# GpSimd's arithmetic moved to VectorE in a two-layer diffusion backbone, with five first feature chunks on TensorE

## The chip, the cores and the metric

The kernel runs on one core of a Trainium2 chip. The metric is the device time of one execution in microseconds; less is better. Engines are named as in the profile: PE is TensorE's matmuls and PEld its weight loads, DVE is VectorE, ACT is ScalarE, POOL is GpSimd, SP is the queue that issues most of the loads. L529 means line 529 of the kernel before.

## The reference, cut to what matters

Two layers over 640 tokens of 1024 features: 128 context tokens (modulated by one condition) and 512 latent tokens (modulated by another). A layer is a feed-forward sublayer, a mixer of four branches with attention, and a second feed-forward sublayer. Each sublayer is wrapped in two norms:

```
def pre(x_, s):
    return rmsnorm(x_, g_pre[l, s]) * (1 + mods[:, 3*s + 1]) + mods[:, 3*s]
f = swiglu(pre(x, 0), w_ffn_gu[l, 0], w_ffn_dn[l, 0])          # (silu(g) * u) @ w_dn
x = x + 0.5 * mods[:, 2] * rmsnorm(f, g_post[l, 0])
m = token_mix(pre(x, 1), ...)   # pooling, spatial gating, latent attention, short conv,
x = x + mods[:, 5] * rmsnorm(m, g_post[l, 1])   # merged by sigmoid gates, one output projection
mods = silu(cond) @ w_mod + b_mod               # nine sections of 1024 per layer
```

## The kernel before, in words

Features lie on partitions, in 8 chunks of 128 (`KC`), and tokens along the free dimension (640, in two halves of 320, `HW`). Every float32 operand is split in a high part (a ScalarE cast) and a low part (a VectorE subtraction, `split`, L242 and L243), and each product is made of three matmuls. Weights come by SP's queue one unit ahead, are split when a task begins (`run`, `advance`), and then the task's function issues its matmuls. All engines work in the order in which the program issues.

**Start** (`start`, L1432 on). The squares of x are summed, and the first two modulation sections are worked out chunk by chunk. Chunks in `BY_PE` use 16 small matmuls each on TensorE (`mod_pe`); the others use dot products along the free dimension (`mod_ve`): three on VectorE (L1496) and one as a GpSimd product (L1502) that ScalarE sums up. `hi` makes the high part of the modulated input (GpSimd product with the norm's factor at L1521, two ScalarE passes, a cast), `lo` the low part (L1528). A `hook` issues these steps between the matmuls of the first three weight units (`first`), so that chunk k is made while chunk k-1 is multiplied.

**Boundaries** (`boundary`, `chain`). Between two sublayers the tokens go half by half. While TensorE runs the tail of one sublayer for the second half, the generator `chain` of the first half is stepped by hand-written counts (`STEPS`): it normalises the branch output f, adds it to x (L450), sums the squares of the new x (L425), and makes the high and low part of the next input (L488 to L509). The second half's chain runs under the next sublayer's head. In `chain`, `scaled` (L414) is a GpSimd product with the norm's factor; a chunk that is `solo` or `alone` has a VectorE form without it. `evac_branch` sums the squares of f (GpSimd, L529), deferred to the next task by `later`. There are five boundaries and a last chain that has a `post` and no `pre`.

**Feed-forward** sublayers make whole-chunk sums of the two input parts for a seven-product scheme (`sums`, L637 on GpSimd). **The mixer** has, in its front, the kv and query norms (`norms`), the rotary key (`rope`), the pooling windows (`windows`, `pooling`), and the short convolution; then 16 attention steps between which gates and branches are filled in, whose outputs are merged by additions (L1127 and L1131 on GpSimd).

GpSimd's queue also issues the transfers of the intermediate results to and from memory.

Of the kernel before, what the change touches and what calls it, by code (L numbers as in the profile page):

```python
# [9 lines left out]
F32 = mybir.dt.float32  # L10
# [18 lines left out]
BY_PE = (0, 2, 4)  # L29
# [51 lines left out]
class Kernel:  # L81
# [319 lines left out]
    def chain(self, hf, ahead, kind, post=None, pre=None, out=None):  # L401
# [15 lines left out]

        accs = (acc,) if ahead else (self.ssq[:, s], acc)
        n = len(accs)

        def square(c, q):
            a = accs[c % n]
            nc.scalar.activation(a if c < n else q, self.x[:, c, s], AF.Square)
            if c >= n:
                (nc.vector if ahead or c % 2 else nc.gpsimd).tensor_add(a, a, q)  # L425

        if post is not None:
# [5 lines left out]
            solo = lambda c: pre is None and not ahead and c in (0, 3)  # L433
# [35 lines left out]

        alone = lambda c: c % 2 == 1  # L470
# [45 lines left out]
    def evac_branch(self, ps, c, hf):  # L516
# [6 lines left out]
        def squares():  # L523
            if c == 0:
                nc.scalar.activation(ssq[:, s], f[:, c, s], AF.Square)
            else:
                q = self.t3()
                nc.scalar.activation(q, f[:, c, s], AF.Square)
                nc.gpsimd.tensor_add(ssq[:, s], ssq[:, s], q)  # L529
# [61 lines left out]
    def ffn(self, l, st, mod_todo, first=False):  # L591
# [35 lines left out]
        def sums():  # L627
# [6 lines left out]
            for k in range(KC // 2):  # L634
                a1, a2, s31, s24 = (self.t6() for _ in range(4))
                for d, c in ((a1, k), (a2, KC // 2 + k)):
                    nc.gpsimd.tensor_add(d, f(self.h[0][:, c, :]), f(self.h[1][:, c, :]))  # L637
# [212 lines left out]
    def mixer(self, l):  # L850
# [36 lines left out]
        def raw_out(name, o, ps, hf):  # L887
# [4 lines left out]
            if sq is not None:  # L892
                d = Z[:, Z_SQ + sq + s.start:Z_SQ + sq + s.stop]
                if name == "cq1":
                    q = self.t3()
                    act.activation(q, ps[:, hf, :HW], AF.Square)
                    pool.tensor_add(d, d, q)
# [49 lines left out]
        def norms():  # L947
# [13 lines left out]
            rope(kr, Z[:, Z_KR:Z_KR + T], segs, pool)  # L961
# [26 lines left out]
        def windows(cc):  # L988
# [3 lines left out]
            pool.tensor_add(s1[:, 1:PADW], x[:, 0:PADW - 1], x[:, 1:PADW])  # L992
            if cc == 0:
                pool.tensor_add(s2[64:128, 2:PADW - 1], s1[64:128, 1:PADW - 2], s1[64:128, 3:PADW])
            else:
                pool.tensor_add(s2[:, 2:PADW - 1], s1[:, 1:PADW - 2], s1[:, 3:PADW])
                pool.tensor_add(s1[:, 4:PADW - 3], s2[:, 2:PADW - 5], s2[:, 6:PADW - 1])
                pool.tensor_add(s2[64:128, 8:PADW - 7], s1[64:128, 4:PADW - 11], s1[64:128, 12:PADW - 3])
            lo, hi = PO, PADW - PO
            pool.tensor_mul(ic[0:64, lo:hi], s1[0:64, lo:hi], ic[0:64, lo:hi])  # L1000
            pool.tensor_mul(ic[64:128, lo:hi], s2[64:128, lo:hi], ic[64:128, lo:hi])

        def pooling(cc):
# [3 lines left out]
            for o, b, n in ((PO, 0, TP), (SO, TP, TS)):  # L1007
                pool.tensor_sub(t[:, b:b + n], ic[:, o:o + n], x[:, o:o + n])
# [62 lines left out]
        def att_begin():  # L1071
# [16 lines left out]
            for b in range(2):  # L1088
                kh, kl = M["kt"][b]
                act.copy(kh[64:96, :], kr[64:96, :])  # L1090
                (dve, pool)[b].tensor_sub(kl[64:96, :], kr[64:96, :], kh[64:96, :].bitcast(F32))
# [18 lines left out]
        def branch(c, i):  # L1110

            def fn(*ws):
# [12 lines left out]
                elif i == 3:  # L1125
                    mg = M["mg"]
                    pool.tensor_add(mg, M["mt"], t)  # L1127
                    pool.dma_start(self.d_acc[c], mg)
                elif i == 1:
                    mg = M["mg"] = M["acc"].pop(c)  # L1130
                    pool.tensor_add(mg, mg, t)  # L1131
# [293 lines left out]
    def build(self):  # L1425
# [6 lines left out]
        def start():  # L1432
# [67 lines left out]
            def mod_ve(c):  # L1500
                t = sp.tile([P, D], F32, tag="pr", name=self.nm("t"), bufs=2)
                nc.gpsimd.tensor_mul(t, loads[0, c], sc[:, 0, :])  # L1502
                dot(1, c, 0)
                dot(1, c, 1)
# [212 lines left out]
```

## Time and profile before

| | |
|---|---|
| median of 3 runs | 3194.71 us (3193.94 to 3196.09) |
| the profiled execution's own time | 3198.12 us |
| its span (first to last instruction) | 3196.3 us |
| mean granted TensorE clock | 0.98 |

The profiled execution is one run more; its span leaves out 1.8 us around the first and the last instruction.

### The profile page before, as it was taken

To read this page: it belongs to the slowest core of one execution; us is meant where nothing else is said; L and a number is where in the kernel's file an instruction comes from. 1 tells how busy PE (TensorE), PEld (TensorE's weight loads), DVE (VectorE), ACT (ScalarE), POOL (GpSimd) and SP (SyncE) were. 2 spreads that over 40 slices of the span, in tenths; PEclk is the share of its full clock that TensorE was granted. 3 is DMA by queue.
4 is the path that set the end of the run, shared out by engine and by line. 5 is a ranking of instruction groups with operands and counts; after the bars stand their busy time and mean duration, and the time that the engine had idled before them with its cause. 6 is when DMAs were issued, how large, how long until landed. Compare 5 with 4: busy or idle time off the path is not lost. (4 is left out here: it accounts for less than half of the span.)

```text
span 3196.3 us, 51354 instructions
## 1 busy us (share of the span) xinstructions
PE 3036.4 (95%) x20278; PEld 2985.0 (93%) x20278; DVE 2353.4 (74%) x3522; ACT 1432.2 (45%) x2535; POOL 653.7 (20%) x601
## 2 busy tenths in 40 slices
PE   7899998999999979999989999989999999899997
PEld 6899997899999979999979999989999998899997
DVE  8978768876656598888688888678666666876665
ACT  4244356454432454443554443563444324544444
POOL 4200025500011242000441000444000113310014
PEclk9999999999999999999999999999999999999999
DMA  4436553311234445446545536542212444445344
GB/s 180 169 120 185 160 170 125 130 59 57 69 107 150 157 152 185 128 136 173 186 151 180 151 114 170 192 160 74 67 49 67 151 139 158 140 141 137 97 141 149
DMA packets 140213, 433.45 MB, mean 136 GB/s; under 512 B 16834, under 2 KB 34050, under 8 KB 139076
## 3 DMA queue, kind: packets, MB, share of 16 engines
q1 hardware_dynamic: 119380, 351.34, 32.8%
q0 software_dynamic: 20304, 78.66, 9.1%
q8 instruction: 159, 2.61, 0.3%
q14 instruction: 82, 0.67, 0.1%
q10 hardware_dynamic: 288, 0.17, 0.0%
HBM read 377.51 MB, written 52.59 MB: 135 GB/s over the span
## 5 line engine op out<-in xcount | busy, mean ns | idle before, releaser
L243 DVE TENSOR_TENSOR wl<-raw,wh 128x1024 fp32r<-128x1024 f32 (+3 forms) x525 | 601.8, 1148 | 380.2 <-ACT wh L242 371.9
L311 PE MATMUL ps<-act,wh 128*128 128x320 f32 x2816 | 567.6, 312 | 33.2 <-ACT act L242 15.4
L242 ACT CAST wh<-raw 128x1024 fp32r<-128x1024 f32 (+3 forms) x525 | 481.1, 919 | 72.6 <-PE ps L311 32.9
L311 PEld LDWEIGHTS ps<-act,wh 128*128 128x128 f32 x2816 | 455.8, 190 | 41.8 <-ACT act L242 18.2
L665 PE MATMUL ps<-s,wh 128*128 128x320 f32 x1920 | 442.9, 310 | 0.5 <-DVE t L689 0.4
L311 PE MATMUL ps<-slotA,wh 128*128 128x320 f32 x1312 | 368.3, 318 | 16.9 <-ACT wh L242 14.0
L311 PE MATMUL ps<-slotD,wh 128*128 128x320 f32 x1312 | 352.5, 316 | 19.5 <-DVE slotD L1528 15.3
L311 PE MATMUL ps<-slotA,wl 128*128 128x320 f32 x1312 | 365.2, 316 | 5.1 <-DVE wl L243 4.8
L311 PE MATMUL ps<-slotB,wh 128*128 128x320 f32 x1312 | 363.5, 315 | 3.0 <-DVE slotB L509 1.6
L311 PE MATMUL ps<-slotC,wh 128*128 128x320 f32 x1312 | 352.0, 316 | 7.4 <-ACT wh L242 3.2
L311 PE MATMUL ps<-act,wl 128*128 128x320 f32 x1408 | 353.7, 311 | 0.0
L375 DVE CUSTOM_DVE_ANT_0 t<-wm,sc,par 128x1024 bf16<-128x1024 f32 x256 | 330.2, 1327 | 12.9 <-DMA wm<-in_w_mod 12.5
L665 PEld LDWEIGHTS ps<-s,wh 128*128 128x128 f32 x1920 | 325.9, 188 | 3.0 <-issue 2.6
L665 PE MATMUL ps<-s,wl 128*128 128x320 f32 x960 | 296.6, 309 | 0.0
L311 PEld LDWEIGHTS ps<-slotA,wh 128*128 128x128 f32 x1312 | 240.5, 193 | 19.9 <-ACT wh L242 15.1
L311 PEld LDWEIGHTS ps<-slotD,wh 128*128 128x128 f32 x1312 | 236.4, 193 | 22.8 <-DVE slotD L1528 16.5
L311 PEld LDWEIGHTS ps<-slotA,wl 128*128 128x128 f32 x1312 | 240.8, 193 | 9.6 <-DVE wl L243 8.4
L311 PEld LDWEIGHTS ps<-act,wl 128*128 128x128 f32 x1408 | 246.3, 190 | 0.2
L311 PEld LDWEIGHTS ps<-slotC,wh 128*128 128x128 f32 x1312 | 236.3, 193 | 9.4 <-ACT wh L242 3.5
L311 PEld LDWEIGHTS ps<-slotB,wh 128*128 128x128 f32 x1312 | 240.7, 193 | 4.4 <-DVE slotB L509 2.2
L311 PE MATMUL ps<-slotC,wl 128*128 128x320 f32 x960 | 239.3, 315 | 1.6 <-DVE wl L243 1.4
L808 POOL DMA_DIRECT2D d_f<-s x64 | 55.3, 864 | 800.4 <-ACT s L804 720.7
(341 smaller groups left out, 6154.3 us busy)
## 6 DMA issues: line engine op xcount, KB each, us to landing
raw<-in_w_gu SPq DMA_DIRECT2D x162, 512.0 KB, 3.9
wm<-in_w_mod SPq DMA_DIRECT2D x144, 512.0 KB, 4.7
raw<-in_w_dn SPq DMA_DIRECT2D x96, 384.0 KB, 3.2
raw<-in_w_gate SPq DMA_DIRECT2D x64, 512.0 KB, 3.6
d_f<-s POOLq DMA_DIRECT2D x96, 320.0 KB, 4.9
ru<-in_w_gu SPq DMA_DIRECT2D x60, 512.0 KB, 5.0
raw<-in_w_in SPq DMA_DIRECT2D x44, 512.0 KB, 3.5
raw<-in_w_dn SPq DMA_DIRECT2D x64, 320.0 KB, 2.9
```

The costliest lines, as they stand in the source:

```text
L242: self.nc.scalar.copy(h, src)
L243: self.nc.vector.tensor_sub(lo, src, h.bitcast(F32))
L311: nc.tensor.matmul(ps[:, hf, :HW], st[:, ws], m[:, k0 + k, hf * HW:(hf + 1) * HW], start=(first and k == 0 and i == 0), stop=(last and k = ...
L375: self.nc.vector.tensor_tensor_reduce(junk, wm, self.sc[:, j, :], 0.5, self.par[l][:, C_BMOD + ch:C_BMOD + ch + 1], ALU.mult, ALU.add, sel ...
L665: nc.tensor.matmul(o, w[x][:, ws], a[y][:, k, :], start=(new and k == 0 and i == 0), stop=(k == n - 1 and i == 2), skip_group_check=not new)
L808: nc.gpsimd.dma_start(self.d_f[c], t, accum_op=ALU.add)
```

## The change

All arithmetic of GpSimd listed in the diff goes to VectorE. In `chain`, each chunk takes the form that had no GpSimd product (`solo` for chains that have a `pre`; `alone` for all chunks), and the squares of x go to one accumulator. In the start, chunks 5 and 7 join those whose modulation TensorE makes; the remaining three have four VectorE dot products; `hi` multiplies gain and norm factor in one VectorE operation per condition and lets ScalarE write the high part directly, and `lo` adds the shift in two pieces. The last chain keeps its GpSimd products for all chunks that are not `solo`; clears and the copy of zeros in `att_begin` stay on GpSimd, and its transfers too.

```diff
--- before.py
+++ after.py
@@ -26,7 +26,7 @@
 NJ = 22
 LAG = 2
 NHEAD = 5
-BY_PE = (0, 2, 4)
+BY_PE = (0, 2, 4, 5, 7)
 PARTS = (5, 5, 6, 6)
 HK = KC // 2 * P
 HEADS = 8
@@ -414,15 +414,14 @@
             nc.gpsimd.tensor_mul(t, src[:, c, s], r)
             return t
 
-
-        accs = (acc,) if ahead else (self.ssq[:, s], acc)
+        accs = (acc,)
         n = len(accs)
 
         def square(c, q):
             a = accs[c % n]
             nc.scalar.activation(a if c < n else q, self.x[:, c, s], AF.Square)
             if c >= n:
-                (nc.vector if ahead or c % 2 else nc.gpsimd).tensor_add(a, a, q)
+                nc.vector.tensor_add(a, a, q)
 
         if post is not None:
             l, st = post
@@ -430,7 +429,7 @@
             r1 = self.R[:, s]
             self.rms_r(r1, (self.ssq[:, s],), 0.25 / D)
 
-            solo = lambda c: pre is None and not ahead and c in (0, 3)
+            solo = lambda c: pre is not None or not ahead and c in (0, 3)
             q1 = lambda c: None if c < KC and solo(c) else scaled(self.f, c, r1)
             nxt = [q1(0), q1(1)]
             yield
@@ -466,8 +465,7 @@
         r2 = self.R[:, s]
         self.rms_r(r2, accs, 1.0 / D)
         late = nxt = None
-
-        alone = lambda c: c % 2 == 1
+        alone = lambda c: True
 
         def first(c):
             return scaled(self.x, c, r2) if c < KC and not alone(c) else None
@@ -526,7 +524,7 @@
             else:
                 q = self.t3()
                 nc.scalar.activation(q, f[:, c, s], AF.Square)
-                nc.gpsimd.tensor_add(ssq[:, s], ssq[:, s], q)
+                nc.vector.tensor_add(ssq[:, s], ssq[:, s], q)
 
         self.later.append(squares)
 
@@ -634,7 +632,7 @@
             for k in range(KC // 2):
                 a1, a2, s31, s24 = (self.t6() for _ in range(4))
                 for d, c in ((a1, k), (a2, KC // 2 + k)):
-                    nc.gpsimd.tensor_add(d, f(self.h[0][:, c, :]), f(self.h[1][:, c, :]))
+                    nc.vector.tensor_add(d, f(self.h[0][:, c, :]), f(self.h[1][:, c, :]))
                 dve.tensor_sub(s31[:, two], a1[:, two], a2[:, two])
                 dve.tensor_sub(s31[:, one], a1[:, one], a1[:, two])
                 dve.tensor_sub(s24[:, one], s31[:, two], a1[:, one])
@@ -894,7 +892,7 @@
                 if name == "cq1":
                     q = self.t3()
                     act.activation(q, ps[:, hf, :HW], AF.Square)
-                    pool.tensor_add(d, d, q)
+                    dve.tensor_add(d, d, q)
                 else:
                     act.activation(d, ps[:, hf, :HW], AF.Square)
 
@@ -958,7 +956,7 @@
             self.split(M["ckvT"][0], M["ckvT"][1], ck)
             pool.dma_start(a["s_ckv"][l], ck[:, 0:TP])
             yield
-            rope(kr, Z[:, Z_KR:Z_KR + T], segs, pool)
+            rope(kr, Z[:, Z_KR:Z_KR + T], segs)
             pool.dma_start(a["s_kr"][l], kr[64:96, 0:TP])
             yield
             r = self.t6()
@@ -989,23 +987,23 @@
             x = zp_buf(cc)
             s1, s2, ic = (M["Z"][:, Z_T + i * PADW:Z_T + (i + 1) * PADW] for i in range(3))
             pool.dma_start(ic, a["icnt"][cc])
-            pool.tensor_add(s1[:, 1:PADW], x[:, 0:PADW - 1], x[:, 1:PADW])
+            dve.tensor_add(s1[:, 1:PADW], x[:, 0:PADW - 1], x[:, 1:PADW])
             if cc == 0:
-                pool.tensor_add(s2[64:128, 2:PADW - 1], s1[64:128, 1:PADW - 2], s1[64:128, 3:PADW])
+                dve.tensor_add(s2[64:128, 2:PADW - 1], s1[64:128, 1:PADW - 2], s1[64:128, 3:PADW])
             else:
-                pool.tensor_add(s2[:, 2:PADW - 1], s1[:, 1:PADW - 2], s1[:, 3:PADW])
-                pool.tensor_add(s1[:, 4:PADW - 3], s2[:, 2:PADW - 5], s2[:, 6:PADW - 1])
-                pool.tensor_add(s2[64:128, 8:PADW - 7], s1[64:128, 4:PADW - 11], s1[64:128, 12:PADW - 3])
+                dve.tensor_add(s2[:, 2:PADW - 1], s1[:, 1:PADW - 2], s1[:, 3:PADW])
+                dve.tensor_add(s1[:, 4:PADW - 3], s2[:, 2:PADW - 5], s2[:, 6:PADW - 1])
+                dve.tensor_add(s2[64:128, 8:PADW - 7], s1[64:128, 4:PADW - 11], s1[64:128, 12:PADW - 3])
             lo, hi = PO, PADW - PO
-            pool.tensor_mul(ic[0:64, lo:hi], s1[0:64, lo:hi], ic[0:64, lo:hi])
-            pool.tensor_mul(ic[64:128, lo:hi], s2[64:128, lo:hi], ic[64:128, lo:hi])
+            dve.tensor_mul(ic[0:64, lo:hi], s1[0:64, lo:hi], ic[0:64, lo:hi])
+            dve.tensor_mul(ic[64:128, lo:hi], s2[64:128, lo:hi], ic[64:128, lo:hi])
 
         def pooling(cc):
             x = zp_buf(cc)
             ic = M["Z"][:, Z_T + 2 * PADW:Z_T + 3 * PADW]
             t = self.t6()
             for o, b, n in ((PO, 0, TP), (SO, TP, TS)):
-                pool.tensor_sub(t[:, b:b + n], ic[:, o:o + n], x[:, o:o + n])
+                dve.tensor_sub(t[:, b:b + n], ic[:, o:o + n], x[:, o:o + n])
             self.split(M["br", 0][0][:, cc, :], M["br", 0][1][:, cc, :], t)
 
         def pool_out(cc):
@@ -1088,7 +1086,7 @@
             for b in range(2):
                 kh, kl = M["kt"][b]
                 act.copy(kh[64:96, :], kr[64:96, :])
-                (dve, pool)[b].tensor_sub(kl[64:96, :], kr[64:96, :], kh[64:96, :].bitcast(F32))
+                dve.tensor_sub(kl[64:96, :], kr[64:96, :], kh[64:96, :].bitcast(F32))
 
 
         G = {}
@@ -1124,11 +1122,11 @@
                     M["mt"] = t
                 elif i == 3:
                     mg = M["mg"]
-                    pool.tensor_add(mg, M["mt"], t)
+                    dve.tensor_add(mg, M["mt"], t)
                     pool.dma_start(self.d_acc[c], mg)
                 elif i == 1:
                     mg = M["mg"] = M["acc"].pop(c)
-                    pool.tensor_add(mg, mg, t)
+                    dve.tensor_add(mg, mg, t)
                     load_acc(c + 2)
                 else:
                     mg = M["mg"]
@@ -1498,13 +1496,9 @@
                     ALU.mult, ALU.add, mod[:, s * KC + c, j:j + 1])
 
             def mod_ve(c):
-                t = sp.tile([P, D], F32, tag="pr", name=self.nm("t"), bufs=2)
-                nc.gpsimd.tensor_mul(t, loads[0, c], sc[:, 0, :])
-                dot(1, c, 0)
-                dot(1, c, 1)
-                dot(0, c, 1)
-                nc.scalar.activation(t, t, AF.Identity, scale=0.5, accum_out=mod[:, c, 0:1])
-                nc.vector.tensor_scalar_add(mod[:, c, 0:1], mod[:, c, 0:1], par[:, C_BMOD + c:C_BMOD + c + 1])
+                for sec in (1, 0):
+                    for j in range(2):
+                        dot(sec, c, j)
                 gain(c, mod[:, KC + c, :])
 
             def squares():
@@ -1516,16 +1510,21 @@
                         nc.vector.tensor_add(sums[c % 2], sums[c % 2], q)
                 nc.vector.tensor_add(acc, *sums)
 
+            conds = ((0, TP, 0), (TP, T, 1))
+
             def hi(c):
                 h = hs[c] = self.t6()
-                nc.gpsimd.tensor_mul(h, self.x[:, c, :], r)
-                for b, e, cd in ((0, TP, 0), (TP, T, 1)):
-                    nc.scalar.activation(h[:, b:e], h[:, b:e], AF.Identity, bias=mod[:, c, cd:cd + 1],
-                                         scale=co[:, 0, c, cd:cd + 1])
-                nc.scalar.copy(self.h[0][:, c, :], h)
+                for b, e, cd in conds:
+                    nc.vector.scalar_tensor_tensor(h[:, b:e], self.x[:, c, b:e], co[:, 0, c, cd:cd + 1], r[:, b:e],
+                                                   op0=ALU.mult, op1=ALU.mult)
+                    nc.scalar.activation(self.h[0][:, c, b:e], h[:, b:e], AF.Identity, bias=mod[:, c, cd:cd + 1])
 
             def lo(c):
-                nc.vector.tensor_sub(self.h[1][:, c, :], hs.pop(c), self.h[0][:, c, :].bitcast(F32))
+                h = hs.pop(c)
+                for b, e, cd in conds:
+                    nc.vector.scalar_tensor_tensor(self.h[1][:, c, b:e], h[:, b:e], mod[:, c, cd:cd + 1],
+                                                   self.h[0][:, c, b:e].bitcast(F32),
+                                                   op0=ALU.add, op1=ALU.subtract)
 
             squares()
             silu()
```

## Rows read from the trace of the kernel before

**Rows 1.** Engine totals of the page: busy us, share of the span, instructions.

```profile
PE 3036.4 (95%) x20278; PEld 2985.0 (93%) x20278; DVE 2353.4 (74%) x3522; ACT 1432.2 (45%) x2535; POOL 653.7 (20%) x601
```

**Rows 2.** Windows: busy us (instructions) of each engine, granted TensorE clock, DMA.

```profile
23.00:76.00 53.00, 37.25 (x196) 35.93 (x196) 50.40 (x60) 20.76 (x34) 32.21 (x13) 0.90 0.32 122
...
480.00:580.00 100.00, 84.06 (x513) 79.55 (x514) 81.83 (x122) 62.62 (x124) 45.70 (x48) 0.95 0.43 142
...
580.00:660.00 80.00, 74.31 (x485) 72.24 (x484) 67.80 (x75) 33.42 (x59) 38.04 (x30) 0.98 0.30 98
...
680.00:900.00 220.00, 219.49 (x1580) 216.92 (x1579) 138.17 (x273) 101.84 (x213) 15.56 (x14) 1.00 0.18 59
```

**Rows 3.** Waits of TensorE, whole span: us in total, times, longest.

```profile
PE ps L311 <- DVE slotD L1528: 15.3, 3, 8.6
...
PE ps L339 <- POOL s L425: 13.9, 5, 3.5
```

**Rows 4.** Timeline of the start: start us, us, engine, line.

```profile
42.20 3.04 POOL L1502 TENSOR_TENSOR t<-wm,sc 128x1024 f32<-128x1024 f32 x1
...
42.92 3.41 DVE L1496 CUSTOM_DVE_ANT_0 junk<-wm,sc,par 128x1024 bf16<-128x1024 f32 x1
...
55.43 1.27 DVE L1496 CUSTOM_DVE_ANT_0 junk<-wm,sc,par 128x1024 bf16<-128x1024 f32 x1
```

**Rows 5.** Groups of VectorE in the start, 23 to 76 us.

```profile
L1496 DVE CUSTOM_DVE_ANT_0 junk<-wm,sc,par 128x1024 bf16<-128x1024 f32 x15 | 30.9, 2060 | 0.4
...
L173 DVE TENSOR_TENSOR wl<-raw,wh 128x1024 fp32r<-128x1024 f32 x3 | 7.0, 2379 | 0.0
...
L1528 DVE TENSOR_TENSOR slotD<-t,slotC 128x640 fp32r<-128x640 f32 x8 | 6.5, 816 | 1.4 <-ACT slotC L1525 1.4
...
L1478 DVE TENSOR_SCALAR co<-mod,par 128x2 f32<-128x2 f32 x8 | 6.1, 762 | 0.0
...
L1507 DVE TENSOR_SCALAR mod<-mod,par 128x1 f32<-128x1 f32 x5 | 1.0, 205 | 0.0
```

**Rows 6.** Groups of VectorE in the first boundary, 480 to 580 us.

```profile
L243 DVE TENSOR_TENSOR wl<-raw,wh 128x1024 fp32r<-128x1024 f32 (+1 forms) x23 | 29.8, 1304 | 8.6 <-ACT wh L242 8.5
...
L450 DVE SCALAR_TENSOR_TENSOR slotA<-t,co,slotA 128x320 f32<-128x320 f32 (+2 forms) x24 | 15.5, 691 | 0.0
...
L505 DVE SCALAR_TENSOR_TENSOR slotD<-t,mod,slotC 128x320 fp32r<-128x320 f32 (+2 forms) x12 | 7.4, 640 | 0.2 <-ACT slotC L490 0.2
...
L488 DVE SCALAR_TENSOR_TENSOR t<-slotA,co,s 128x320 f32<-128x320 f32 (+2 forms) x12 | 7.3, 633 | 0.0
```

**Rows 7.** Groups of VectorE in the first mixer's front, 580 to 660 us.

```profile
L243 DVE TENSOR_TENSOR wl<-raw,wh 128x1024 fp32r<-128x1024 f32 x10 | 14.9, 1495 | 5.7 <-ACT wh L242 5.4
...
L327 DVE SCALAR_TENSOR_TENSOR t<-t,t 128x640 f32<-128x640 f32 x2 | 4.3, 2152 | 0.1
...
L326 DVE SCALAR_TENSOR_TENSOR t<-t,t 128x640 f32<-128x640 f32 x2 | 3.9, 1962 | 0.1
...
L325 DVE SCALAR_TENSOR_TENSOR t<-t,t 128x640 f32<-128x640 f32 x2 | 3.0, 1503 | 0.0
```

**Rows 8.** Timeline of VectorE at places without GpSimd arithmetic.

```profile
92.35 0.48 DVE L638 TENSOR_TENSOR t<-t,t 128x320 f32<-128x320 f32 x1
...
500.00 0.54 DVE L450 SCALAR_TENSOR_TENSOR slotA<-t,co,slotA 128x320 f32<-128x320 f32 x1
...
503.20 0.95 DVE L243 TENSOR_TENSOR wl<-raw,wh 128x768 fp32r<-128x768 f32 x1
...
550.00 1.21 DVE L243 TENSOR_TENSOR wl<-raw,wh 128x1024 fp32r<-128x1024 f32 x1
...
569.81 0.67 DVE L488 SCALAR_TENSOR_TENSOR t<-slotA,co,s 128x128 f32<-128x128 f32 x2
```

**Rows 9.** Timeline of the start, TensorE's modulation of one chunk.

```profile
44.51 3.83 PE L1486 MATMUL ps<-cf,wm 128*128 128x2 f32 x32
```

**Rows 10.** Groups of GpSimd: count, busy us, mean ns, idle before, releaser.

```profile
L529 POOL TENSOR_TENSOR s<-s,t 128x320 f32<-128x320 f32 x84 | 112.9, 1344 | 177.7 <-ACT t L528 177.7
```

## The prediction

> **What bounds the kernel now.** I read the page's engine totals first [rows 1]: TensorE is busy for 3036.4 of 3196.3 us, so about 160 us are idle, and VectorE for 2353.4, or 74%. An average says little here, so I cut the span into stretches of 20 us and looked for those where TensorE drops. They are the start (0 to 160), the five boundaries between sublayers, the front of the two mixers, and the tail. The table of stretches [rows 2] shows them beside a quiet one: in the start VectorE is busy 50.4 of 53 us while TensorE has 37.25, in the first boundary 81.8 of 100 against 84.1, in the mixer's front 67.8 of 80; in the attention, 680 to 900, TensorE has 219.5 of 220 and VectorE only 138. So gains can come from the first three kinds of place alone, and what is put on VectorE in the attention lies under TensorE's work. TensorE's list of waits [rows 3] names who ends them: in the start VectorE's low parts (L1528, 15.3 us in three waits), in the boundaries the square sums (L425), 13.9 us of them by GpSimd.
>
> The second reading is what VectorE's time in these places consists of. The timeline of the start [rows 4] shows one dot product of 1024 columns (L1496) taking 3.41 us while a GpSimd product runs, and the same instruction 1.27 us once none runs. The groups of the start [rows 5] put that on all 15 dots (mean 2060 ns), on three weight splits (2379 ns), and on an operation of two columns (762 ns). The boundary's and the mixer front's groups [rows 6, 7] are stretched likewise against their clean neighbours [rows 8]. **The trace so says that GpSimd's arithmetic is not a second pair of hands: while it runs, VectorE's instructions with two SBUF operands last about as long as the two would in turn.**
>
> The Trainium skill, page "SBUF — State Buffer", section "Who interferes with whom", says that a VectorE instruction with two SBUF inputs contends with a GpSimd instruction that reads SBUF, the second to issue being blocked. The 3.41 against 1.27 us agree with it.
>
> **The change, part by part.** *Start.* Clean prices: dot 1.27, weight split 1.21, 640 columns 0.82, and 0.21 for an operation of one or two columns (L1507's mean) [rows 4, 5, 8]. VectorE runs nearly without a pause from 23 to 76 us [rows 2]. What it loses: 15 dots x (2.06 - 1.27) = 11.9; three of 15 dots and their extra additions, since chunks 5 and 7 go to TensorE and VectorE's three chunks have four dots instead of three, 3 x 1.27 + 1.0 = 4.8; splits 3 x (2.38 - 1.21) = 3.5; gains (L1478) 8 x (0.76 - 0.21) = 4.4; together 24.6. What it gets: per chunk the product with the gain over 128 and 512 columns and the low part in two pieces, about 2 x 1.0 in place of 0.82, so 8 x 1.15 = 9.2, and two more pairs of bias additions, 0.5. VectorE ends 14.9 us earlier, near 61 us. TensorE can't follow all the way: two more chunks of modulation at 3.83 us each [rows 9] stand in its queue between products, 7.7 us, of which the 15.3 us of waits cover all but the last chunk's (it stands before k=4, where the low part is nearly ready). I take -10 for this piece (bounds: -15 if TensorE hides both, -7 if neither). The following 76 to 144 us are VectorE's too; the eight whole-token sums (L637) go to it at 0.82 each, 6.6, and if each stretched what ran beside it as a weight split was stretched above, by 1.17, that gives back 9.4. I count -2 (bounds -3 and +6.6, the latter if they stretched nothing). Start: -12.
>
> *Boundaries.* For the first one, 480 to 580 us, by groups [rows 6] against clean prices [rows 8]. Gone: L450 15.5 - (8 x 0.54 + 8 x 0.67) = 5.8; L505 and L488 7.4 + 7.3 - 2 x (4 x 0.54 + 4 x 0.67) = 5.0; weight splits 23 x 1.304 - (15 x 1.21 + 8 x 0.95) = 4.2. Sum 15.0; smaller groups are left out. Added: the 16 residual additions of 320 columns that the form without GpSimd needs, 16 x 0.48 = 7.7; the even chunks of the second norm, which had GpSimd's product, 4 x (2 x 0.54 - 0.48) in the half of one piece and 4 x (2 x 0.67 - 0.82) in the half of two (0.34 for the piece of 128 columns, worked out from the pair's 0.67, and 0.48 for the low part), 4.5; four squares 1.9; seven sums of branch squares (L529) and one for the query norm 3.8. Sum 17.9. By these rows the ledger closes to +3, and the smaller groups and the overlap of neighbouring instructions eat most of it. So VectorE's load stays, and what is left to win is what passes through GpSimd on the path: squares at 13.9/5 = 2.8 us of TensorE's wait per boundary [rows 3], now three VectorE additions, and ScalarE's second cast per even chunk. Against it, the second half's last norm is paced by VectorE at 1.3 us a chunk instead of about 1.1. I take -1 a boundary (bounds -5 and +4), -5 for five.
>
> The 84 sums of branch squares cost GpSimd 112.9 us and it waited 177.7 us for ScalarE in front of them [rows 10]. On VectorE they stand behind the weight split of the same task, which takes 0.95 us [rows 8]. The ScalarE square that they need is issued right behind that split's cast and runs over 320 columns against the split's 768, so it is there when the split ends: no wait of their own, and in the first half of each tail, where only one half's branch runs, VectorE has room. If that cover is missing, see the first rival.
>
> *Mixer front* (twice). Gone [rows 7]: splits 10 x (1.495 - 1.21) = 2.9; three of the norm chain's steps, L327, L326 and L325, 2 x (2.15 + 1.96 + 1.50 - 3 x 0.82) = 6.3; sum 9.2 from these rows, and the other stretched groups are not counted. Added: ten window operations of about 0.84, two pooling differences in two pieces (2 x 0.97), the key rope (about 2.6) and one low part (0.95), 13.9; but half of the windows comes behind the pooled low part that TensorE waits for, and that low part no longer queues behind a stretched norm chain. The table load (L991) is issued by an otherwise idle queue, ahead of the products that need it. I take -2.5 each (bounds -6 and +4): -5.
>
> *Merges.* 32 additions of 640 columns, 32 x 0.82 = 26 us, under TensorE's full stretches [rows 2]; nothing. Uncovered they cost 26.
>
> *The end.* The last norm chain keeps its GpSimd products (the condition exempts only chains with a following norm), so its stretch stays; the last sum of branch squares, at 0.48 instead of GpSimd's 1.34 or less [rows 8, 10], saves under a microsecond; I take 0.4.
>
> Sum: -12 - 5 - 5 - 0.4 = -22.4 against the profiled execution's own 3198.1 us (span 3196.3 and 1.8 around it), 3175.7. That execution lies 3.4 above the median of the runs, 3194.7, so **3172 us** there.
>
> **Rivals.** (1) *A slower one: VectorE's order.* The sums of branch squares stand in VectorE's queue, and where ScalarE's square is late, the weight split of the next task stands behind it and TensorE behind that. Some 35 of the 84 lie in the busy half of the five boundaries; GpSimd waited 177.7/84 = 2.1 us each [rows 10]. At 1.2 us each, that is +42: 3214. It decides from 22.4/35 = 0.64 us each. Against it: the split's length covers the square. 7%.
> (2) *No change.* VectorE's ledger in the boundaries and fronts stays open at +3 and +5, some of which TensorE sees, and the start's gain is halved by the two chunks on TensorE: -7 + 1 = -6, about 3189 of the runs' median, and up to the old time. 14%.
> (3) *More.* Every removed wait also gives back TensorE's clock, granted at 0.90 to 0.95 in these stretches and 1.00 in the attention [rows 2]: full clock over the 53 us of the start and 100 us of each boundary would be another 5 + 5 x 5. With half of that, 15, and -3 a boundary instead of -1, 10: 3172 - 25 = 3147. 18%.
> (4) *VectorE is simply full.* If the long instructions are long for another reason, nothing is given back, and 17.9 x 5 + 13.9 x 2 = 117 us come onto an engine with some 18 us to spare in a boundary [rows 2]; half of it shown gives 3250. The clean runs beside GpSimd's idle time speak against it. 3%.
>
> Beside (4): the Trainium skill, page "Perfetto Trace Analysis", section "Optimizing Scalar/DVE Operations", says that where VectorE is saturated, moving work to other engines, even GpSimd, may make sense, with the reserve that the two share a port. By the first half of that rule this change goes the wrong way, towards (4); by the reserve it goes the right way, as [rows 4] has it.
>
> **Numbers.** Forecast 58%. A change of 0.2%, 6.4 us, is about what a measurement of this kernel can tell. Faster by more: forecast, (3) and a little of (2), 0.78; within: most of (2) and the forecast's edge, 0.13; slower: (1), (4) and the edge, 0.09. The range of 3147 to 3194 reaches to (3) on one side and the unchanged time on the other.
>
> **What would show it.** Dots at 1.27 and gains at 0.21 us throughout; the first product's last low part near 61 us instead of 76; no VectorE group of one shape far above its clean price except at the end; L425 and L450 without GpSimd around them; VectorE's total within some 30 us of 2353. The prediction is wrong if TensorE waits in the tails on splits queued behind L529, or if the start ends later than 70 us because of TensorE's own modulation.

## The result and the profile after

The changed kernel takes 3175.69 us (median of four runs, 3171.82 to 3177.40) beside 3194.85 for the kernel before on the same chip (3193.94 to 3196.09): ratio 0.9932, 95% interval 0.9919 to 0.9944, that is 18 to 26 us less. The profiled execution took 3175.49 us, span 3173.7, at a mean granted clock of 0.981 (0.980 before). Against the profiled execution of before that is -22.6 us, between the medians it is -19.2; the terms of the prediction add up to -22.4. The sum fits, and its parts don't.

Engine totals of the page, after (to be held against [rows 1]):

```profile
PE 3040.3 (96%) x20332; PEld 2993.2 (94%) x20332; DVE 2354.0 (74%) x3889; ACT 1409.4 (44%) x2497; POOL 158.8 (5%) x263
```

GpSimd is left with DMA issues, clears and the last chain, and VectorE has 367 instructions more in the same busy time: 2354.0 against 2353.4 us. What it took over is paid by what is no longer stretched. I compared each VectorE instruction that overlaps GpSimd arithmetic with the median of its line and shape elsewhere: some 185 to 190 us of stretch before, 8.5 after, nearly all of that in the last chain.

The windows of [rows 2] in the changed kernel (same columns):

```profile
23.00:76.00 53.00, 48.92 (x256) 48.43 (x257) 36.92 (x78) 9.00 (x16) 0.00 (x0) 0.90 0.33 124
480.00:580.00 100.00, 85.81 (x516) 80.52 (x515) 80.41 (x162) 60.92 (x121) 3.13 (x14) 0.93 0.45 151
580.00:660.00 80.00, 74.64 (x498) 73.98 (x497) 65.32 (x99) 32.16 (x58) 3.19 (x9) 0.96 0.26 82
680.00:900.00 220.00, 219.61 (x1590) 217.56 (x1589) 145.02 (x281) 103.47 (x216) 3.80 (x7) 1.00 0.17 57
```

In the start the roles have changed over: TensorE is busy 48.92 us of 53 in place of 37.25, VectorE 36.92 in place of 50.40. The granted clock of these three stretches has not risen (0.90, 0.93, 0.96 for 0.90, 0.95, 0.98).

VectorE's groups after, in the start (the dots, the weight splits and the gains, to [rows 5]) and in the first boundary (the splits and the residual product, to [rows 6]):

```profile
L1494 DVE CUSTOM_DVE_ANT_0 junk<-wm,sc,par 128x1024 bf16<-128x1024 f32 x12 | 15.4, 1283 | 0.3
L173 DVE TENSOR_TENSOR wl<-raw,wh 128x1024 fp32r<-128x1024 f32 x3 | 3.5, 1216 | 0.0
L1476 DVE TENSOR_SCALAR co<-mod,par 128x2 f32<-128x2 f32 x8 | 1.8, 222 | 0.0
```

```profile
L243 DVE TENSOR_TENSOR wl<-raw,wh 128x1024 fp32r<-128x1024 f32 x15 | 18.2, 1222 | 8.5 <-ACT wh L242 8.5
L446 DVE SCALAR_TENSOR_TENSOR t<-slotB,co,s 128x320 f32<-128x320 f32 x8 | 4.4, 545 | 0.0
```

Dots at 1.28 us (2.06 before), splits at 1.22 (2.38 in the start), gains at 0.22 (0.76): the clean prices of the prediction.

TensorE's waits after (to [rows 3]):

```profile
PE ps L339 <- DVE s L424: 35.5, 10, 4.3
...
PE ps L311 <- ACT br L242: 12.4, 4, 5.4
...
PE ps L311 <- DVE wl L243: 8.0, 13, 0.9
...
PE ps L311 <- DVE slotD L1525: 3.6, 1, 3.6
```

The 15.3 us of waits for the start's low parts have become 3.6. The wait for the square sums has not become smaller: 35.5 us in ten waits, where it had been 13.9 in five for GpSimd's additions [rows 3] and 16.8 in six for VectorE's:

```profile
PE ps L339 <- DVE s L425: 16.8, 6, 5.5
```

To see where the time came from I matched the matmuls of each trace with those of before, in order, by their tiles, and cut at the same matmuls. The first column is the stage's length before; then the change of its length in the kernel after, and in brackets the change of TensorE's idle time in it; then the change of length in six experiments (below). F is a feed-forward sublayer, M a mixer; FM1 is the first boundary from F to M. The feed-forward bodies between these stages, where no column moves by more than 1 us, are left out.

```
us                 before  after (idle)   start  chain  sums  chain+sums  idle prod.  repairs
first product        79.3   +1.0 (-11.2)   -0.0   +0.3  +0.6     +0.3       -2.7      -7.7
whole-token sums     85.9   -4.3  (-3.7)   +0.0   +0.1  -3.3     -3.4       -3.1      -3.9
FM1                 129.9   -1.2  (-1.9)   +0.1   +3.3  +0.2     +1.3       +9.3      -6.5
front of mixer 1     84.9   -0.9  (-0.2)   +0.3   -1.0  +0.0     +0.0       -0.3      -0.3
MF1                 215.4   -3.0  (-4.7)   +2.0   -0.7  -2.6     -4.3       +6.4      -6.5
FF                  205.1   -2.5  (-1.8)   +1.2   +1.2  -4.0     -6.6       +9.4      -9.3
FM2                 135.0   -1.3  (-1.2)   -0.1   +2.5  +0.5     -0.9       +7.8      -5.6
front of mixer 2    120.3   -2.3  (+0.9)   +0.3   -1.0  -0.8     -0.9       -1.7      -1.5
MF2                 225.2   -7.8  (-3.1)   -2.6   -3.0  -4.0     -7.3       +3.3      -9.6
two attentions      705.0   -0.7  (-0.1)   +0.0   +0.0  -0.1     +0.2       -0.6      -0.7
end                 106.3   +0.2  (+0.4)   -0.1   +1.2  -0.8     +1.8       -0.8      -0.8
```

One execution stands behind each column. Boundaries in which a kernel changed nothing moved by up to 2.6 us (MF2 in the start's column), so a single entry is good to some 3 us; the verdicts below are those of the medians. The first product is the loosest: the new start stands unchanged in five more of the kernels below, and there it moved by +1.2, -2.7, -2.7, +0.4 and -0.2 us.

### The profile page after: what moved, and what is told of

The parts are those of the page before. It is cut to its first block, busy times and chain, and to the rows that moved or that the text cites. A ratio compares the mean times of both kernels' runs of the same rounds, so it can differ in the third digit from the quotient of the medians.

```text
span 3173.7 us, 51228 instructions
## 1 busy us (share of the span) xinstructions
PE 3040.3 (96%) x20332; PEld 2993.2 (94%) x20332; DVE 2354.0 (74%) x3889; ACT 1409.4 (44%) x2497; POOL 158.8 (5%) x263
## 5 line engine op out<-in xcount | busy, mean ns | idle before, releaser
L243 DVE TENSOR_TENSOR wl<-raw,wh 128x1024 fp32r<-128x1024 f32 (+3 forms) x525 | 557.9, 1065 | 365.2 <-ACT wh L242 357.9
L311 PEld LDWEIGHTS ps<-act,wh 128*128 128x128 f32 x2816 | 458.0, 190 | 33.3 <-ACT act L242 16.8
L375 DVE CUSTOM_DVE_ANT_0 t<-wm,sc,par 128x1024 bf16<-128x1024 f32 x256 | 318.1, 1280 | 5.1 <-DMA wm<-in_w_mod 4.8
L802 ACT COPY s<-ps 128x640 f32<-128x640 f32 x96 | 66.6, 694 | 292.0 <-issue 185.6
```

What stands on the lines that cost most here:

```text
L243: self.nc.vector.tensor_sub(lo, src, h.bitcast(F32))
L311: nc.tensor.matmul(ps[:, hf, :HW], st[:, ws], m[:, k0 + k, hf * HW:(hf + 1) * HW], start=(first and k == 0 and i == 0), stop=(last and k = ...
L375: self.nc.vector.tensor_tensor_reduce(junk, wm, self.sc[:, j, :], 0.5, self.par[l][:, C_BMOD + ch:C_BMOD + ch + 1], ALU.mult, ALU.add, sel ...
L802: nc.scalar.copy(t.rearrange("p (a b) -> p a b", a=2), ps[:, :, :HW])
```

## The experiments

Ratios are to the kernel before, from runs on the same chip; in us they are taken at its 3194.85. Inserted lines shift the line numbers of some kernels.

**The start alone.** The kernel before with `BY_PE`, `mod_ve`, `hi` and `lo` of the changed one.

> The kernel before with the new start alone (five chunks of the first modulation on TensorE, the other three wholly on VectorE, new high and low parts); all else as before. By the prediction's own terms this is worth -10 for the first product and nothing more, since the eight whole-token sums stay on GpSimd: about 3185 us, ratio 0.997. The rival, from the trace of the changed kernel, where TensorE runs without a pause from 36 to 79 us: the two more chunks on TensorE (3.9 us each, and half clock behind each) eat what VectorE gives back, the first product ends at the old place, 79 us, and the stage is worth 0 to -2: about 3194 us, ratio within 0.999 to 1.000.

Measured: 3194.42 us (before 3197.21), ratio 0.9989 (0.9980 to 0.9998), -0.6 to -6.4 us. In the trace the first product ends where it ended before (-0.04 us) although TensorE's idle time in it fell by 10.8. The rival is nearer; the interval's upper half holds it.

**Three chunks on TensorE.**

```
-BY_PE = (0, 2, 4, 5, 7)
+BY_PE = (0, 2, 4)
```

> The changed kernel with three first chunks on TensorE as before (0, 2 and 4) and five wholly on VectorE. If the prediction was right that VectorE's work sets the start and TensorE's added chunks are covered, eight more dots at 1.28 us make the first product end some 7 us later: slower, 3180 to 3183 us. The rival: TensorE's own modulation sets it now. Then the first product ends at about 75 us in place of 79.5, because VectorE, which pauses for 9.7 us in the changed kernel, takes the dots into that pause: 3 to 5 us faster than the changed kernel, about 3172 us.

Measured: 3170.95 us, ratio 0.9919 (0.9906 to 0.9933): beside the changed kernel's 0.9932 no difference that the intervals hold, surely not some 7 us slower. Neither account of the mechanism fits: the first product ends at 79.5 us here and at 80.3 with five, cut at the matmul that comes at 79.3 before, and a single trace can't tell these apart. VectorE has its last low part ready at 72.2 us, TensorE is idle for 19.9 of the 79.5 us in place of 11.9 of 80.3, and at the end both ways are equally long.

**The chains alone.** The kernel before with the residual, the second norm and the square sums off GpSimd (four lines of `chain`).

> The kernel before with the norm chains alone off GpSimd (residual products, second norm's products, square sums); the sums of branch squares, mixer front, merges and start as before. By the prediction's terms: -5 over the five boundaries, about 3190 us, ratio 0.9984. The rival, from the aligned traces of before and after (TensorE's matmuls come 15.6 us earlier over the five boundaries): the chains carry most of the change, -10 to -16, about 3182 us, ratio 0.995 to 0.997.

Measured: 3194.50 us, ratio 0.9998 (0.9989 to 1.0007): nothing. The rival is gone, and the prediction's -5 (0.9984) lies just outside the interval. VectorE's busy time is 2346.1 us, 7.3 less than before: what the chains put on VectorE is very nearly what they stop stretching, as the ledger of the prediction had it (15.0 gone and 17.9 added in a boundary, 3.8 of it for sums that stay on GpSimd here).

**The sums of branch squares back on GpSimd.** In the changed kernel, `nc.vector.tensor_add(ssq[:, s], ssq[:, s], q)` on `nc.gpsimd` again.

> The changed kernel with the 70 sums of branch squares (and the end's) back on GpSimd. If sums in VectorE's queue hold up the splits behind them (the prediction's first rival) this is faster than the changed kernel by 0.3 us or more for each of some 35 sums, that is 3165 us or less. If they are covered, as the prediction had it, nothing is won by moving them back, and what GpSimd's additions stretch beside them costs 0 to 5 us: 3176 to 3181 us.

Measured: 3174.07 us, ratio 0.9926 (0.9914 to 0.9939), the same as the changed kernel. They are covered on either engine. VectorE's total is 16.3 us lower here, 2337.7, for 84 additions of 0.48 us, some 40 us, given away; by these totals the rest came back as longer instructions.

**One line: the whole-token sums.** The stage table shows 4.3 us won between 79 and 165 us, where in the kernels so far only the changed `sums` differs.

```
-    nc.gpsimd.tensor_add(d, f(self.h[0][:, c, :]), f(self.h[1][:, c, :]))
+    nc.vector.tensor_add(d, f(self.h[0][:, c, :]), f(self.h[1][:, c, :]))
```

> The kernel before with one line changed: the 32 whole-token additions of the four 'sums' (L637; eight for each feed-forward stage) on VectorE. By the prediction they were worth -2 in the start and nothing elsewhere: about 3193 us, ratio 0.9994. The new theory, from the stage table (79 to 165 us became 4.3 us shorter only in the kernels that have this line; mixer to feed-forward 3.0 and 7.8, feed-forward to feed-forward 2.5 shorter, where the chains alone gave 0.7, 3.0 and -1.2): -4 in the start and -1 to -3 at each of three boundaries, -7 to -12 in all, 3183 to 3188 us, ratio 0.996 to 0.998. A second rival, that no part gives anything until GpSimd is wholly idle: 0 to -3.

Measured: 3186.38 us (before 3195.46), ratio 0.9967 (0.9955 to 0.9980), -6 to -14 us. One line makes about half of the change's gain: -3.3 us in the start, -2.6, -4.0 and -4.0 where a feed-forward sublayer follows. The same stretch of VectorE, first before with GpSimd's line under it, then here (start us, duration, engine, line):

```profile
121.45 1.29 DVE L375 CUSTOM_DVE_ANT_0 t<-wm,sc,par 128x1024 bf16<-128x1024 f32 x1
122.66 2.60 DVE L375 CUSTOM_DVE_ANT_0 t<-wm,sc,par 128x1024 bf16<-128x1024 f32 x1
125.18 2.19 DVE L243 TENSOR_TENSOR wl<-raw,wh 128x640 fp32r<-128x640 f32 x1
...
121.68 5.01 POOL L637 TENSOR_TENSOR t<-slotC,slotD 128x640 f32<-128x640 f32 x2 [13.12 <-DVE mod L375]
```

```profile
122.84 1.28 DVE L375 CUSTOM_DVE_ANT_0 t<-wm,sc,par 128x1024 bf16<-128x1024 f32 x1
124.05 0.82 DVE L243 TENSOR_TENSOR wl<-raw,wh 128x640 fp32r<-128x640 f32 x1
...
125.52 1.56 DVE L637 TENSOR_TENSOR t<-slotC,slotD 128x640 f32<-128x640 f32 x2
```

Two additions held GpSimd for 5.01 us and cost VectorE (2.60 - 1.28) + (2.19 - 0.82) = 2.7 us; done by VectorE itself they take 1.56. VectorE's total fell by 9.1 us, to 2344.3, with 32 instructions more.

**The same line back** in the changed kernel.

> The changed kernel with the same 32 additions back on GpSimd, and nothing else. If they carry -7 to -12 by themselves, this gives it back: 3182 to 3188 us. If they are worth what the prediction said, 3177 to 3179. If the gain needs all of GpSimd idle, most of the 21 us is lost: 3188 us or more.

Measured: 3183.95 us, ratio 0.9962 (0.9949 to 0.9976): 9.6 us of the gain is gone.

**The mixer fronts alone.** The kernel before with `rope`, `windows`, `pooling`, the query norm's sum and the keys' low part on VectorE.

> The kernel before with the two mixer fronts alone off GpSimd (key rope, pooling windows and differences, one sum of the query norm, one low part of the keys). By the prediction's terms -5 for both, bounds -12 and +8: about 3190 us, ratio 0.9984. From the stage table of the changed kernel (0.9 and 2.3 us shorter, but with more idle time of TensorE in the second): -1 to -3, ratio about 0.9995, and TensorE's wait in front of the pooling product (3.1 us before, 5.4 us in the changed kernel) is 5 us here too, since half of the windows now stands ahead of that low part on VectorE.

Measured: 3196.24 us, ratio 1.0001 (0.9992 to 1.0010): nothing won. TensorE's waits at the pooling product were 3.1 and 1.1 us and are one of 5.2 us.

**Idle products.** In the changed kernel, GpSimd computes 120 products that nobody reads, where the chains had theirs.

```
+    if pre is not None:
+        nc.gpsimd.tensor_mul(self.junk, self.f[:, c, s.start:s.start + 312], r1[:, :312])
...
+    if c % 2 == 0:
+        nc.gpsimd.tensor_mul(self.junk, self.x[:, c, s.start:s.start + 312], r2[:, :312])
```

> The changed kernel with 120 GpSimd products (24 for each of the five boundaries that have a following norm, as many as the kernel before had there, of 312 columns) whose result nothing reads; they wait only for their inputs. If the cost of GpSimd's arithmetic is what it stretches on VectorE, VectorE's instructions beside them get longer by 0.5 to 1.2 us each, and with VectorE busy for eight tenths of a boundary that is 2 to 8 us at each: 3186 to 3215 us. If GpSimd costs only where another engine waits for its result, nothing changes: 3174 to 3178 us.

Measured: 3230.50 us, ratio 1.0105 (1.0092 to 1.0119), 55 us above the changed kernel. Engine totals of its page:

```profile
PE 3048.9 (95%) x20332; PEld 3000.7 (93%) x20332; DVE 2415.7 (75%) x3889; ACT 1410.3 (44%) x2497; POOL 288.5 (9%) x383
```

And its timeline, eight of the products and what VectorE does under them:

```profile
479.46 9.27 POOL L443 TENSOR_TENSOR junk<-slotB,s 128x312 f32<-128x312 f32 x8 [30.27 <-DVE s L330]
...
482.14 1.15 DVE L449 SCALAR_TENSOR_TENSOR t<-slotB,co,s 128x320 f32<-128x320 f32 x1
483.32 1.04 DVE L454 TENSOR_TENSOR slotA<-slotA,t 128x320 f32<-128x320 f32 x1
...
486.41 0.47 DVE L718 SCALAR_TENSOR_TENSOR t<-t,ps 128x320 f32<-128x320 f32 x1
...
489.52 0.54 DVE L449 SCALAR_TENSOR_TENSOR t<-slotB,co,s 128x320 f32<-128x320 f32 x1
490.10 0.49 DVE L454 TENSOR_TENSOR slotA<-slotA,t 128x320 f32<-128x320 f32 x1
```

The residual product takes 1.15 us under the products and 0.54 behind them, the addition 1.04 and 0.49; L718, whose second operand is in PSUM, keeps its 0.47. No engine's wait is ended by one of these products, and no transfer that another engine needs became later (ScalarE's weight casts wait 14.3 us for their loads, 18.4 in the changed kernel). What grows are TensorE's waits for VectorE (to be held against 35.5 and 8.0 above):

```profile
PE ps L340 <- DVE s L425: 42.7, 10, 5.7
PE ps L312 <- DVE wl L244: 20.4, 21, 2.7
```

VectorE's total rises by 61.7 us and the time by 55 between the medians, by 49 between the two profiled executions. The stretching alone is the cost.

**Idle copies**: the same places and size, one operand (`nc.gpsimd.tensor_copy(self.junk, r1[:, :312])`, and `r2`).

> As the kernel with 120 idle GpSimd products (3230.5 us), but each product of two operands replaced by a copy of one operand, of the same 312 columns and at the same places; the result is read by nobody. If any arithmetic of GpSimd stretches VectorE, it costs about as much: 3210 to 3235 us. If it needs two operands read from SBUF on GpSimd's side, the time is that of the changed kernel plus a few us: 3174 to 3182 us.

Measured: 3184.64 us, ratio 0.9968 (0.9955 to 0.9981), 11.5 us above the changed kernel: a fifth of the products' price, and just above the second expectation. VectorE's total rises by 16.9 us. Its timeline under eight of the copies:

```profile
483.16 6.07 POOL L443 COPY junk<-s 128x312 f32<-128x312 f32 x8 [31.98 <-DVE s L330]
...
484.98 0.72 DVE L449 SCALAR_TENSOR_TENSOR t<-slotB,co,s 128x320 f32<-128x320 f32 x1
485.74 0.62 DVE L454 TENSOR_TENSOR slotA<-slotA,t 128x320 f32<-128x320 f32 x1
```

**Idle products in the attention**: 128 of them, two behind each gate product of the merges (`pool.tensor_mul(self.junk, t[:, 0:312], t[:, 312:624])`).

> The changed kernel with 128 idle GpSimd products of 312 columns, two behind each of the 64 gate products of the merges, where TensorE is busy without pause. If it is the place that decides, VectorE's busy time grows by some 40 to 70 us as with the 120 products in the boundaries, and the time stays: 3174 to 3180 us. If stretched instructions on VectorE cost wherever they stand, about as much as there, +55: 3230 us.

Measured: 3182.06 us, ratio 0.9951 (0.9939 to 0.9964), 6.1 us above the changed kernel, about as much as two such intervals leave open, and 2 us above the first expectation. VectorE's total rises by 38.4 us; a microsecond of it costs 0.16 us here against 0.8 to 0.9 in the boundaries. Matched by stages, 3.8 us of it lie in the two attentions. The window shows the cover: TensorE stays full.

```profile
680.00:900.00 220.00, 218.39 (x1570) 215.40 (x1570) 148.40 (x279) 102.17 (x215) 35.76 (x35) 1.00 0.18 57
```

**Chains and whole-token sums together.**

> The kernel before with the norm chains and the whole-token sums off GpSimd, start, mixer fronts, merges and sums of branch squares as before. Alone they gave ratio 0.9998 and 0.9967. If the parts add, 0.9965: 3184 us. If part of the change's gain is made only where both stand beside each other (the boundaries into a feed-forward stage, where one part left on GpSimd still stretches what the other moved to VectorE), more: 0.994 to 0.995, 3176 to 3180 us.

Measured: 3184.09 us (before 3198.64), ratio 0.9960 (0.9946 to 0.9974). The parts add: 0.9965 was expected from the two alone. With the start (-0.11%) and the mixer fronts (+0.01%) that makes -0.50% of the change's -0.68%; the rest lies within the intervals, and the merges, which no run had alone, show -0.7 us in the attentions.

**Three repairs** of the changed kernel: four chunks on TensorE, none beside another; the second pooling difference before the last convolution; and a norm's last two squares left to TensorE.

```
-BY_PE = (0, 2, 4, 5, 7)
+BY_PE = (0, 2, 4, 6)
...
-            if c >= n:
+            if c >= KC - 2:
+                extra.append(q)
+            elif c >= n:
                 nc.vector.tensor_add(a, a, q)
...
-        self.rms_r(r2, accs, 1.0 / D)
+        self.rms_r(r2, (*accs, *extra), 1.0 / D)
...
-  Task("windows", lambda: windows(1)), pool_out(0), conv_out(1, 1), Task("pooling", lambda: pooling(1)),
+  Task("windows", lambda: windows(1)), Task("pooling", lambda: pooling(1)), pool_out(0), conv_out(1, 1),
```

> The changed kernel with three edits where its trace still shows TensorE waiting: four first chunks on TensorE, none beside another (0, 2, 4, 6); the second pooling difference moved ahead of the last convolution product's task; and the squares of a norm's last two chunks not added on VectorE but left to TensorE, which sums them with two more matmuls of 0.43 us while it waits anyway. From the traces: start -1 to -3; pooling -2 each of two; TensorE's ten waits for the square sums (3.5 us each) shorter by one addition of 0.48 us and its hand-over, -0.7 each, -7 in all. 3163 to 3169 us. Rival: the waits only move to the next thing that is late (ScalarE's last square, its weight casts), then 3172 to 3176 us.

Measured: **3145.87 us** (before 3195.41), ratio 0.9842 (0.9829 to 0.9854): 50 us faster than before and 29 than the changed kernel, more than expected. TensorE's waits:

```profile
PE ps L339 <- DVE s L427: 16.3, 7, 3.1
...
PE ps L311 <- ACT swh L242: 10.9, 2, 5.5
...
PE ps L339 <- ACT t L423: 2.5, 3, 0.8
```

The square sums cost 16.3 + 2.5 us in place of 35.5, and the five boundaries are 21.7 us shorter than in the changed kernel (stage table, FM1 to MF2), where of the three repairs only that of the squares acts. The first product is 8.7 shorter. Some 3.7 of that need not be the repair: chunk 4 took 3.82 us here and 6.82 in the changed kernel (the next section tells why), and two kernels with the start of the changed one and a chunk 4 of 3.8 to 4.2 us moved by -2.7 in place of +1.0. The pooling repair only changed the name of the wait: 5.5 us for the cast of the small weight unit in place of 5.4 for the pooled input.

## Why the prediction was right in sum, and where its steps failed

**The sum is luck, the cause is not.** The start gave 8.7 us less than its -12, the boundaries 10.8 more than their -5, the rest some 2 less than forecast; only the total agrees. That GpSimd's arithmetic is no second pair of hands in a full stage is shown by the idle products: no result is waited for, and VectorE grows by 62 us and the kernel by 55. The clean prices were met to some hundredths of a microsecond, and VectorE's total came within 0.6 us of the old one, where 30 were allowed.

**Start: -12 predicted, -3.3 measured; of this the first product -10 predicted, +1.0 measured.** The step that failed is "7.7 us, of which the 15.3 us of waits cover all but the last chunk's". The waits went as predicted (TensorE's idle time -11.2 us), and TensorE's own work took their place (+12.2). The prediction named this case among its signs: the start ends later than 70 us because of TensorE's own modulation, and by that sign this part is wrong. The timeline of TensorE's modulation, chunks 0 and 2 in the kernel before, then chunks 4, 5 and 7 in the changed kernel with VectorE's wait and its last low parts:

```profile
16.46 6.83 PE L1486 MATMUL ps<-cf,wm 128*128 128x2 f32 x32
...
23.73 6.99 PE L1486 MATMUL ps<-cf,wm 128*128 128x2 f32 x32 [0.44 <-DVE mod L1490]
```

```profile
39.97 6.82 PE L1484 MATMUL ps<-cf,wm 128*128 128x2 f32 x32
...
51.43 3.92 PE L1484 MATMUL ps<-cf,wm 128*128 128x2 f32 x32
...
61.84 4.07 PE L1484 MATMUL ps<-cf,wm 128*128 128x2 f32 x32
...
55.38 0.34 DVE L1488 TENSOR_SCALAR mod<-ps,par 128x2 f32<-128x2 f32 x2 [9.69 <-PE ps L1484]
...
68.88 1.93 DVE L1525 SCALAR_TENSOR_TENSOR slotD<-t,mod,slotC 128x128 fp32r<-128x128 f32 x4
```

The two added chunks cost 8.0 us, as priced, and chunk 4 took 3.0 more than the 3.83 of before [rows 9]. That makes 11.0 of the 12.2. The 3.83 was the lowest of three prices in the trace of before: chunks 0 and 2 took 6.83 and 6.99. Which of the two a chunk costs goes with TensorE's clock. In the kernel with the idle copies chunk 5 lies wholly in a stretch with a granted clock of 0.50, the 1.2 GHz level, and takes 6.82 (us, TensorE, its weight loads, VectorE, ScalarE and GpSimd busy, granted clock, DMA share, GB/s):

```profile
48.60:55.40 6.80, 6.80 (x34) 6.80 (x33) 0.00 (x0) 0.00 (x0) 0.00 (x0) 0.50 0.00 0
```

Around chunk 4 of the changed kernel the pairs of 320-column matmuls start 0.53 us apart, as they do at a granted 0.50 behind chunk 7, and not 0.29 as at 1.00 from 72 us on; so it ran at the lower level too. The clock column shows 1.00 there, but the trace's first clock entry stands only at 51 us. Of the six other kernels with five chunks, chunk 4 took 6.82 in three (first product +1.2, -0.0 and -0.2) and 3.8 to 4.2 in three (-2.7, -2.7 and +0.4; the last is the one whose chunk 5 took 6.82). So the first product moved by +1.2 to -2.7 us, by the luck of the clock, and never by -10. Why the higher level comes at 40 us in some executions and at 51 in others stays open.

The windows behind chunk 7 (us, TensorE busy and matmuls, granted clock, DMA share, GB/s):

```profile
65.80:71.60 5.80, 5.80 (x23) 0.50 0.00 0
71.60:79.50 7.90, 7.90 (x54) 0.99 0.00 0
```

23 matmuls take 5.8 us at a granted clock of 0.50, then 54 take 7.9 at 0.99; at the later pace the 23 take 3.4. Against the kernel before this is hardly a loss: from 23 to 76 us its granted clock was 0.90 too, and the matmuls of the first product other than the modulation's took only 1 to 2 us longer in all. Also, VectorE stands still for 9.69 us: chunk 5's matmuls were issued ahead of the reading of chunk 4's result, and the trace shows that this reading began only when they had ended (51.43 + 3.92 = 55.35). VectorE so ended at 70.8 us, not at 61.

**76 to 144 us: -2 predicted, -4.3 measured**, -3.3 by the one-line kernel. The direction was right; the 9.4 us of stretch that go were undersized.

**Boundaries: -1 each predicted.** The two into a mixer gave -1.2 and -1.3. The three into a feed-forward sublayer gave -3.0, -2.5 and -7.8, -13.3 together, for a predicted -3. The failed step is an omission: the prediction counted the eight whole-token sums of the start and not the other 24, which each later feed-forward sublayer makes in its first tasks, on a VectorE that is busy for 87, 88 and 69% of the time there (1205 to 1260, 1696 to 1726 and 2770 to 2830 us before). The one-line kernel puts -10.6 there. Of the -7.8, TensorE's idle time makes only 3.1; the rest is its own work, and kernels that change nothing there moved by -1.0 and -2.6, so some of it is the one execution of before. The chains, to which the prediction gave these five microseconds, gave none (0.9998): TensorE's wait for the square sums was 30.7 us before, 13.9 of it for GpSimd, and is 37.4 with the chains alone on VectorE, so what was to be won there was not.

**Mixer fronts: -5 predicted, -3.2 in the stage table, and nothing by themselves** (1.0001). What went from the norm chain came back in front of the pooled input, which TensorE now waits for 5.4 us.

**Merges: 0 predicted**, -0.7 measured. They also explain how VectorE's total can stand still while the time falls: in 740 us of the two attentions (690 to 1090 and 2300 to 2640 before, 685 to 1085 and 2285 to 2625 after) its busy time rose from 471.4 to 486.9 us, where the idle products cost 0.16 us per microsecond, so the other places were relieved by about 15. That the merges are that work is argued from the totals, not shown by a run of the merges alone.

**The rivals.** The slower one (sums of branch squares hold up the splits) is ruled out by moving them back: 0.9926 against 0.9932. The second, no change, is ruled out by the interval, and a full VectorE by its total. That the clock comes back did not happen (0.981 against 0.980), but with the three repairs some of it did (0.987). The Trainium skill, page "Perfetto Trace Analysis", section "Optimizing Scalar/DVE Operations", which the prediction weighed, is borne out in its reserve and not in its first half: the one-line kernel moves work to the busier engine and gains 6 to 14 us.

## What to carry to other kernels

Price an addition on GpSimd by what it stretches on VectorE beside it, not by GpSimd's own idle time: in a full stage two of 640 columns cost VectorE 2.7 us there and 1.56 if it did them itself. Ask for every place in which a moved line runs, not only for the one that is being looked at; here three quarters of the line that mattered lay elsewhere. And when a wait of TensorE goes because work was moved to TensorE, add up TensorE's work again, at the price that it has at the lower clock as well: one chunk cost 3.8 or 6.8 us.

## What the hardware showed that was not expected

A GpSimd copy with one SBUF operand also stretches VectorE, less than a product: 0.72 and 1.15 us for an instruction of 0.55. The Trainium skill, page "SBUF — State Buffer", section "Who interferes with whom", names a GpSimd instruction that reads SBUF, so a copy falls under its rule; the trace agrees that both kinds cost, and shows that the price is not the same. In the changed kernel a chunk's matmuls of two columns were followed by matmuls at a granted clock of 0.50 for some 6 us, with no wait between them (the windows behind chunk 7); that the two columns are the reason is not shown. And leaving the last two squares of each norm to TensorE, in place of two additions of 0.48 us, shortened the boundaries by 21.7 us, three times the 7 that were expected; TensorE's idle time makes 16.2 of them, about what its waits for the sums fell by (35.5 to 18.8), and its own work 5.5, although it has 40 more matmuls: the granted clock of the five boundaries is 0.96 to 0.99 there, against 0.95 to 0.97 in the changed kernel.
